# Block transposes over 128 partitions, with a trip through HBM that orders their rows

## The chip, the cores and the metric

The kernel runs on one core of one Trainium2 chip. TensorE (PE in the profile) does the matmuls, VectorE (DVE) and ScalarE (ACT) the elementwise work, GpSimd (POOL) here memsets and a few DMA issues, SyncE (SP) issues nearly all DMAs. The metric is the device time of one execution in microseconds (us). Three runs of the kernel before took 2368.86, 2369.55 and 2369.81 us; the median is 2369.55 us.

## The reference

Two models of two layers each run one after the other on one sequence of 256 tokens with 1024 channels, all in float32. Every layer is a half-weighted SwiGLU feed-forward network (FFN), a mixer with attention, and a second FFN; each begins with an RMS norm. There are eight FFNs in all, and they hold most of the work:

```
def swiglu(x, w_in, w_out):            # w_in: 1024 x 5632, w_out: 2816 x 1024
    g, u = jnp.split(x @ w_in, 2, axis=-1)
    return (jax.nn.silu(g) * u) @ w_out

for l in range(DEPTH):                 # the first model; the second has another mixer
    x = x + 0.5 * swiglu(rms_norm(x, ffn1_norm[l]), ffn1_w_in[l], ffn1_w_out[l])
    x = x + mixer(rms_norm(x, mix_norm[l]), ...)    # q, k, v = h @ w_in: attention, and a Fourier branch
    x = x + 0.5 * swiglu(rms_norm(x, ffn2_norm[l]), ffn2_w_in[l], ffn2_w_out[l])
```

## The kernel before

Tokens lie on the partitions: x is one tile of 128 partitions x 2 token halves (t) x 1024 channels. A matmul needs the channels on the partitions, so the activations are transposed and then split into two parts, hi (rounded to fp32r) and lo (the remainder): xhi and xlo for x, hhi and hlo for the hidden layer h of an FFN. ACT makes hi, DVE makes lo (`split`, L313). Weights are split in the same way while they stream in, and every product is three matmuls, hi x hi, lo x hi and hi x lo (`mm3`, L112 to L116).

`unit` (L80) loads 1 MB of weights (4 blocks of 128 rows x 512 columns) into a `raw` buffer, of which there are four, and splits it in two halves of 128x1024 elements: whi on ACT (L315), wlo on DVE (L316). Such a half feeds 12 matmuls of 512 columns (2 row blocks x 2 token halves x 3). Inside an FFN four halves can be held at a time: two buffers of the pools `whi` and `wlo`, and two more that `more(2)` grants.

An FFN (`ffn`, L218) goes through six column blocks c of the hidden layer (the last is half as wide). For each it does the gate and the up product (16 weight blocks), then ACT takes the silu (L246) and DVE the product h (L248). h is transposed in four groups that begin at the blocks 0, 2, 4 and 5, with 8, 8, 4 and 2 pieces of 128 channels (nk). `queue_t` (L65) puts the transposes of a group and then its splits into a list, `todo`. `unit` takes up to `rate` = 4 entries from it after each weight half and ties them behind that half's wlo on DVE (L104 to L106); `drain` takes all that are left.

`queue_blocks` (L179) does the transposes: DVE transposes 32x32 blocks within 32 partitions, so each instruction reads 32 partitions of the source and writes 32 partitions of the target at the place where the block belongs; that makes 16 instructions of 32 partitions x nk*32 elements for each token half, 32 for a group. For the first 512 channels of x after an FFN `queue_x` (L170) does the same with nk = 4; the other 512 are transposed on PE (`xt_half`, L187). In the first model's mixer (`mixer1`, L418) q and k are transposed in this way too, into qT and kT (L456), and are split after the four projections (L470 to L474).

The tile framework orders the instructions of each engine from a simulated timeline; each engine then works strictly in that order. hhi goes to ACT's list, hlo and wlo to DVE's.

Of the kernel before, what the change touches and what calls it, by code (L numbers as in the profile page):

```python
# [10 lines left out]
F32 = mybir.dt.float32  # L11
# [7 lines left out]
P = 128  # L19
T = 2  # L20
# [6 lines left out]
class Net:  # L27
    def __init__(self, tc, ctx, a):
        self.tc, self.nc, self.a = tc, tc.nc, a
        nc = self.nc  # L30
        pool = lambda n, b, **kw: ctx.enter_context(tc.tile_pool(name=n, bufs=b, **kw))
# [9 lines left out]
        self.at = pool("at", 4, space=PS)  # L41
        self.tp = pool("tp", 1, space=PS)
        self.uid = 0
        self.flip = False
# [13 lines left out]
        self.hold = False  # L58
        self.todo, self.rate = [], 4

# [4 lines left out]
    def queue_t(self, h, nk, hhi, hlo, k0):  # L65
        hv = self.b("hT", n=2048)[:, : nk * 256].rearrange("p (k t) -> p k t", k=nk)
        for t in range(T):
            self.queue_blocks(h[t], nk, hv, t)
        for i in range(0, nk, 2):
            self.todo.append(lambda i=i: self.split(hhi[:, k0 + i : k0 + i + 2], hlo[:, k0 + i : k0 + i + 2],  # L70
                                                    hv[:, i : i + 2]))

# [97 lines left out]
    def queue_x(self, li):  # L170
        nc = self.nc
        hv = self.xtile()[:, :1024].rearrange("p (k t) -> p k t", k=4)
        for t in range(T):
            self.queue_blocks(self.x[:, t, :512], 4, hv, t)
        for k in range(4):
            g = self.gcol[:, li, k : k + 1] if isinstance(li, int) else li[:, k : k + 1]
            self.todo.append(lambda k=k, g=g: self.split(self.xhi[:, k], self.xlo[:, k], hv[:, k], scale=g))

    def queue_blocks(self, src, nk, hv, t):  # L179
        src = src.rearrange("p (k c i) -> p k c i", c=4, i=32)  # L180
        for q in range(16):
            qa, qc = q // 4, q % 4
            self.todo.append(lambda qa=qa, qc=qc: self.nc.vector.transpose(  # L183
                (hv(qc) if callable(hv) else hv)[32 * qc : 32 * qc + 32, :, t * P + 32 * qa : t * P + 32 * qa + 32],
                src[32 * qa : 32 * qa + 32, :nk, qc, :]))

# [196 lines left out]
class Mix1:  # L383
# [34 lines left out]
    def mixer1(self, l, nxt):  # L418
        nc, a, tc = self.nc, self.a, self.tc
# [3 lines left out]
        big = self.big  # L423
        self.more(2)
        tl = lambda n, sh, dt=F32: big.tile(sh, dt, name=self.nm(n), tag="m1" + n)
        kzh = big.tile([P, 4, 2, 256], F32R, name=self.nm("kzh"), tag="mlo")
        kq = big.tile([P, 4096], F32R, name=self.nm("kq"), tag="m1th")
        kzl = kq[:, :2048].rearrange("p (k i t) -> p k i t", k=4, i=2)
        ql = kq[:, 2048:3072].rearrange("p (k t) -> p k t", k=4)
        qT = big.tile([P, 4, 256], F32, name=self.nm("qT"), tag="m1fhi")  # L430
        kT = big.tile([P, 4, 256], F32, name=self.nm("kT"), tag="m1flo")
        qh, vn = tl("qh", [P, 4, 256], F32R), tl("vn", [P, T, 512])
# [6 lines left out]
        for c in range(4):  # L439
# [5 lines left out]
            if c < 2:  # L445
                h = []
                for t in range(T):
# [6 lines left out]
                    h.append(ht)  # L454
                for t in range(T):
                    self.queue_blocks(h[t], 4, qT if c == 0 else kT, t)  # L456
            elif c == 2:
# [12 lines left out]
        self.drain()  # L470
        self.split(qh, ql, qT)
        for i in range(2):
            r = slice(64 * i, 64 * i + 64)
            self.split(kzh[r, :, i, :], kzl[r, :, i, :], kT[r])  # L474
        ohi, olo = tl("ohi", [P, 4, 256], F32R), tl("olo", [P, 4, 256], F32R)
# [19 lines left out]
        for g in range(4):  # L495
            pa = self.psum(self.at)
            for tt in range(T):
                s = slice(g * P, (g + 1) * P)
# [5 lines left out]
            for q in range(2):  # L504
                s = slice(q * P, (q + 1) * P)
# [9 lines left out]
        for c in range(4):  # L515
# [4 lines left out]
            for t in range(T):  # L520
                d = th[:, t, c * 512 : (c + 1) * 512]
# [618 lines left out]
```

## Time and profile before

| | |
|---|---|
| runs, median of 3 | 2369.55 us (2368.86 to 2369.81) |
| profiled execution, its span | 2366.5 us |
| between the two | 3.05 us outside the span or from run to run; the profile has no other time of its own |
| PE busy | 2291.0 us, 97% of the span |
| DVE busy | 1891.9 us, 80% |
| ACT busy | 1144.7 us, 48% |
| POOL busy | 22.3 us, 1% |
| DMA | 407.07 MB, mean 172 GB/s; 16 engines busy about half of the time |

The span runs from the first to the last instruction of the profiled execution. A busy PE is not a PE at its full rate: an instruction's bar lasts 0.39 us, while the starts of two matmuls of 512 columns are 0.23 us apart where nothing is late. So what PE loses is read from its waits and from the number of matmuls in a stretch, not from the busy share. DVE's share is an average too: it differs a good deal between stretches.

### The profile page before, as it was taken

Reading aid. Unit: us, or ns where it says so; the run is one execution under the profiler, and the core shown is the slowest. Engines: PE = TensorE matmul, PEld = TensorE weight load, DVE = VectorE, ACT = ScalarE, POOL = GpSimd, SP = SyncE. Lnnn points to the kernel's source line nnn. Section 1 sums busy time; section 2 is a strip of 40 time slices with the busy share of each in tenths; the row PEclk is TensorE's granted clock in tenths of the full one; section 3 lists DMA queues with packets and bytes.
Section 4 is the critical chain, followed back from the end, with each engine's and each line's share of the span. In section 5 each row is a group of like instructions: output and inputs, shape, how many; then the busy total and the mean of one; then the engine's idle time right before and its main releaser. Section 6 shows DMA issues by size and latency. Waiting matters only on the chain.

```text
span 2366.5 us, 28600 instructions
## 1 busy us (share of the span) xinstructions
PE 2291.0 (97%) x10446; PEld 1846.8 (78%) x10446; DVE 1891.9 (80%) x3797; ACT 1144.7 (48%) x1632; POOL 22.3 (1%) x47
## 2 busy tenths in 40 slices
PE   8999999999999999999999999999999999999999
PEld 7777788778778788777777887787787788778777
DVE  6898866896798876798788896768958978877785
ACT  5444445445444455445444655544444455455443
POOL 0000000000000000000000000000000000000000
PEclk9999999999999999999999999999999999999999
DMA  7555555556546645546555544455464555325553
GB/s 257 177 171 185 177 170 178 173 174 201 182 151 200 191 152 178 189 142 219 176 175 179 174 125 132 137 185 182 166 211 161 173 191 156 124 96 189 185 177 117
DMA packets 228269, 407.07 MB, mean 172 GB/s; under 512 B 20800, under 2 KB 46016, under 8 KB 228128
## 3 DMA queue, kind: packets, MB, share of 16 engines
q1 hardware_dynamic: 212272, 397.44, 51.0%
q10 hardware_dynamic: 14944, 4.79, 0.9%
q0 software_dynamic: 912, 3.02, 0.5%
q8 instruction: 82, 1.34, 0.2%
q14 instruction: 59, 0.48, 0.1%
HBM read 404.16 MB, written 1.05 MB: 171 GB/s over the span
## 4 chain that ended last, share of the span: by engine, by line
PE 66%; DVE 27%; issue 5%; ACT 2%; DMA 1%; ACTq 0%; DVEq 0%
PE ps L115 20%; PE ps L116 20%; PE ps L114 19%; DVE hT L183 14%; DVE wlo L316 8%; DVE h L248 2%; PE ps L377 2%; DVE hlo L316 1%; ACT whi L315 1%; PE ps L370 1%; PE ps L863 1%; DVE qT L183 1%; PE ps L655 1%; DMA raw<-in_mix_w_in_dram 1%; PE ps L194 1%
## 5 line engine op out<-in xcount | busy, mean ns | idle before, releaser
L315 ACT CAST whi<-raw 128x1024 fp32r<-128x1024 f32 (+2 forms) x754 | 780.2, 1043 | 834.4 <-PE ps L116 744.8
L316 DVE TENSOR_TENSOR wlo<-raw,whi 128x1024 fp32r<-128x1024 f32 (+2 forms) x754 | 907.6, 1213 | 337.1 <-ACT whi L315 323.6
L115 PE MATMUL ps<-wlo,xhi 128*128 128x512 f32 (+2 forms) x2048 | 804.6, 394 | 14.7 <-DVE wlo L316 14.7
L114 PE MATMUL ps<-whi,xhi 128*128 128x512 f32 (+2 forms) x2048 | 772.4, 394 | 22.1 <-DVE h L248 18.9
L116 PE MATMUL ps<-whi,xlo 128*128 128x512 f32 (+2 forms) x2048 | 791.2, 390 | 0.0
L114 PEld LDWEIGHTS ps<-whi,xhi 128*128 128x128 f32 x2048 | 383.4, 188 | 112.7 <-DVE h L248 25.7
L115 PEld LDWEIGHTS ps<-wlo,xhi 128*128 128x128 f32 x2048 | 384.8, 188 | 110.5 <-DVE wlo L316 31.2
L116 PEld LDWEIGHTS ps<-whi,xlo 128*128 128x128 f32 x2048 | 384.8, 188 | 79.3 <-issue 0.5
L183 DVE STREAM_TRANSPOSE hT<-h 32x256 f32<-32x256 f32 (+2 forms) x1024 | 360.8, 352 | 15.4
L115 PE MATMUL ps<-wlo,hhi 128*128 128x512 f32 x704 | 279.1, 396 | 23.7 <-DVE wlo L316 23.7
L116 PE MATMUL ps<-whi,hlo 128*128 128x512 f32 x704 | 275.8, 392 | 0.0
L114 PE MATMUL ps<-whi,hhi 128*128 128x512 f32 x704 | 266.2, 392 | 1.1 <-DVE h L248 0.2
L115 PEld LDWEIGHTS ps<-wlo,hhi 128*128 128x128 f32 x704 | 132.1, 188 | 65.2 <-DVE wlo L316 37.5
L114 PEld LDWEIGHTS ps<-whi,hhi 128*128 128x128 f32 x704 | 132.2, 188 | 33.7 <-DVE h L248 4.6
L116 PEld LDWEIGHTS ps<-whi,hlo 128*128 128x128 f32 x704 | 132.2, 188 | 27.8
L315 ACT CAST hhi<-hT 128x512 fp32r<-128x512 f32 x88 | 49.1, 618 | 119.1 <-DVE hT L183 119.1
L246 ACT ACTIVATE sl<-ps,rstd 128x512 f32<-128x512 f32 (+1 forms) x96 | 62.3, 651 | 56.4 <-PE ps L116 52.3
L183 DVE STREAM_TRANSPOSE hT<-x 32x128 f32<-32x128 f32 x224 | 67.7, 302 | 3.4
L365 ACT ACTIVATE pr<-ms,nmx 128x256 f32<-128x256 f32 (+1 forms) x112 | 51.3, 461 | 34.0 <-DVE nmx L360 29.9
L248 DVE SCALAR_TENSOR_TENSOR h<-ps,rstd,sl 128x512 f32<-128x512 f32 (+1 forms) x96 | 64.7, 700 | 1.9 <-PE ps L116 1.6
L316 DVE TENSOR_TENSOR hlo<-hT,hhi 128x512 fp32r<-128x512 f32 x88 | 55.7, 685 | 0.3
L137 ACT ACTIVATE jk<-x 128x512 f32<-128x512 f32 x52 | 32.7, 630 | 5.3 <-DVE x L299 2.6
(350 smaller groups left out, 1681.7 us busy)
## 6 DMA issues: line engine op xcount, KB each, us to landing
raw<-in_ffn_w_gu_dram SPq DMA_DIRECT2D x80, 1024.0 KB, 5.1
raw<-in_ffn_w_in_dram SPq DMA_DIRECT2D x79, 1024.0 KB, 5.2
raw<-in_ffn_w_out_dram SPq DMA_DIRECT2D x40, 1024.0 KB, 5.0
raw<-in_ffn_w_down_dram SPq DMA_DIRECT2D x40, 1024.0 KB, 5.1
raw<-in_mix_w_in_dram SPq DMA_DIRECT2D x32, 1024.0 KB, 6.7
raw<-in_w_gate_dram SPq DMA_DIRECT2D x24, 1024.0 KB, 5.1
raw<-in_w_in_dram SPq DMA_DIRECT2D x12, 1024.0 KB, 5.5
raw<-in_ffn_w_in_dram SPq DMA_DIRECT2D x16, 512.0 KB, 4.6
```

The source lines that it names most:

```text
L114: mm(ps[:, :n], lhsT=lh, rhs=hi, start=start, stop=False)
L115: mm(ps[:, :n], lhsT=lh, rhs=lo, start=False, stop=False)
L116: mm(ps[:, :n], lhsT=ll, rhs=hi, start=False, stop=stop)
L137: self.nc.scalar.activation(junk, self.x[:, t, n * 512 : (n + 1) * 512], AF.Square, accum_out=ss[:, t, n : n + 1])
L183: self.todo.append(lambda qa=qa, qc=qc: self.nc.vector.transpose((hv(qc) if callable(hv) else hv)[32 * qc : 32 * qc + 32, :, t * P + 32 * ...
L194: nc.tensor.transpose(ps[:, j * 256 + t * P : j * 256 + (t + 1) * P], self.x[:, t, k * P : (k + 1) * P], self.ident)
L246: nc.scalar.activation(sl[:, :w], gs[t][:, :w], AF.Silu, scale=rs[:, t : t + 1])
L248: nc.vector.scalar_tensor_tensor(h[t][:, o : o + w], us[t][:, :w], rs[:, t : t + 1], sl[:, :w], op0=ALU.mult, op1=ALU.mult)
L315: self.nc.scalar.copy(hi, src)
L316: return self.nc.vector.tensor_sub(lo, src, hi.bitcast(F32))
L365: nc.scalar.activation(pr[:, s], src[:, s], AF.Exp, bias=nm[:, j : j + 1], accum_out=den[:, j : j + 1])
L377: nc.tensor.matmul(po[:, j * 64 : (j + 1) * 64], lhsT=pt[:, q], rhs=v(j, st), start=(st == 0), stop=(st == ns - 1))
```

## The change

The 16 transposes of 32 partitions for each token half become one instruction over all 128 partitions (`turn` in the new function `turned`, which takes the place of `queue_blocks`). It transposes each 32x32 block where it stands: the four quarters of the token half stay in their own 32 partitions, and the channels are taken with a step of four elements. What it writes, a tile hB, has the right elements in the wrong partitions. Two DMAs issued on POOL's queue put that right: the first writes hB to a buffer in HBM (`hop`), the second reads it back with the rows in order into the tile that the transposes wrote before (hT, qT or kT). Both move 1 MB for nk = 8, 512 KB for nk = 4 and 256 KB for nk = 2.

hT then has its columns in another order (quarter, piece, token half), and the splits read it in runs of 32 elements, one token half at a time, four pieces at a time: as many splits as before for nk = 8 and nk = 4, two of half the width in place of one for nk = 2, eight of 128x128 in place of four of 128x256 for x, and twice as many of half the width for q and k. `rate` goes from 4 to 1, and empty entries in the list (two for h, three for x) leave weight halves between the transposes and the splits.

```
@@ -40,6 +40,7 @@
         self.acc = pool("acc", 3, space=PS)
         self.at = pool("at", 4, space=PS)
         self.tp = pool("tp", 1, space=PS)
+        self.hop = pool("hop", 2, space=bass.MemoryType.DRAM)
         self.uid = 0
         self.flip = False
         self.ident = self.cst.tile([P, P], F32, name="ident")
@@ -56,19 +57,38 @@
         self.extra = self.turn = 0
         self.lead = True
         self.hold = False
-        self.todo, self.rate = [], 4
+        self.todo, self.rate = [], 1
 
     def drain(self):
         while self.todo:
             self.todo.pop(0)()
 
     def queue_t(self, h, nk, hhi, hlo, k0):
-        hv = self.b("hT", n=2048)[:, : nk * 256].rearrange("p (k t) -> p k t", k=nk)
-        for t in range(T):
-            self.queue_blocks(h[t], nk, hv, t)
-        for i in range(0, nk, 2):
-            self.todo.append(lambda i=i: self.split(hhi[:, k0 + i : k0 + i + 2], hlo[:, k0 + i : k0 + i + 2],
-                                                    hv[:, i : i + 2]))
+        hv = self.turned(lambda t: h[t], nk, self.b("hT", n=2048))
+        self.todo += [lambda: None] * 2
+        step = min(nk, 4)
+        for i in range(0, nk, step):
+            for t in range(T):
+                o = lambda d: d[:, k0 + i : k0 + i + step, t * P : (t + 1) * P].rearrange(
+                    "p k (q j) -> p k q j", j=32)
+                self.todo.append(lambda hi=o(hhi), lo=o(hlo), s=hv[:, i : i + step, t]: self.split(hi, lo, s))
+
+    def turned(self, src, nk, tile):
+        nc = self.nc
+        n = nk * 256
+        hop = self.hop.tile([4, P, nk * 64], F32, name=self.nm("hop"), tag=f"hop{nk}")
+        hb = self.b("hB", n=2048, bufs=1)[:, :n]
+        ov = hb.rearrange("p (c k t j) -> p k c t j", c=4, t=T, j=32)
+
+        def turn(t):
+            nc.vector.transpose(ov[:, :, :, t, :], src(t)[:, : nk * P].rearrange("p (k i c) -> p k c i", c=4, i=32))
+            if t == T - 1:
+                nc.gpsimd.dma_start(out=hop.rearrange("q (i c) n -> (q i) (c n)", c=4), in_=hb)
+                nc.gpsimd.dma_start(out=tile[:, :n].rearrange("p (q n) -> p q n", q=4),
+                                    in_=hop.rearrange("q p n -> p q n"))
+
+        self.todo += [lambda t=t: turn(t) for t in range(T)]
+        return tile[:, :n].rearrange("p (q k t j) -> p k t q j", q=4, t=T, j=32)
 
     def nm(self, s):
         self.uid += 1
@@ -168,21 +188,16 @@
         return r
 
     def queue_x(self, li):
-        nc = self.nc
-        hv = self.xtile()[:, :1024].rearrange("p (k t) -> p k t", k=4)
-        for t in range(T):
-            self.queue_blocks(self.x[:, t, :512], 4, hv, t)
-        for k in range(4):
+        hv = self.turned(lambda t: self.x[:, t, :512], 4, self.xtile())
+        self.todo += [lambda: None] * 3
+
+        def part(k):
             g = self.gcol[:, li, k : k + 1] if isinstance(li, int) else li[:, k : k + 1]
-            self.todo.append(lambda k=k, g=g: self.split(self.xhi[:, k], self.xlo[:, k], hv[:, k], scale=g))
-
-    def queue_blocks(self, src, nk, hv, t):
-        src = src.rearrange("p (k c i) -> p k c i", c=4, i=32)
-        for q in range(16):
-            qa, qc = q // 4, q % 4
-            self.todo.append(lambda qa=qa, qc=qc: self.nc.vector.transpose(
-                (hv(qc) if callable(hv) else hv)[32 * qc : 32 * qc + 32, :, t * P + 32 * qa : t * P + 32 * qa + 32],
-                src[32 * qa : 32 * qa + 32, :nk, qc, :]))
+            for t in range(T):
+                o = lambda d: d[:, k, t * P : (t + 1) * P].rearrange("p (q j) -> p q j", j=32)
+                self.split(o(self.xhi), o(self.xlo), hv[:, k, t], scale=g)
+
+        self.todo += [lambda k=k: part(k) for k in range(4)]
 
     def xt_half(self, n, li):
         nc = self.nc
@@ -427,8 +442,8 @@
         kq = big.tile([P, 4096], F32R, name=self.nm("kq"), tag="m1th")
         kzl = kq[:, :2048].rearrange("p (k i t) -> p k i t", k=4, i=2)
         ql = kq[:, 2048:3072].rearrange("p (k t) -> p k t", k=4)
-        qT = big.tile([P, 4, 256], F32, name=self.nm("qT"), tag="m1fhi")
-        kT = big.tile([P, 4, 256], F32, name=self.nm("kT"), tag="m1flo")
+        qT = big.tile([P, 1024], F32, name=self.nm("qT"), tag="m1fhi")
+        kT = big.tile([P, 1024], F32, name=self.nm("kT"), tag="m1flo")
         qh, vn = tl("qh", [P, 4, 256], F32R), tl("vn", [P, T, 512])
         u = big.tile([P, KD, 256], F32R, name=self.nm("u"), tag="mhi").rearrange("p (h t a) b -> p h t (a b)", h=2, t=2)
         uhi, ulo = u[:, 0], u[:, 1]
@@ -452,8 +467,8 @@
                     else:
                         nc.vector.tensor_scalar(out=ht, in0=ps[t], scalar1=sc, scalar2=None, op0=ALU.mult)
                     h.append(ht)
-                for t in range(T):
-                    self.queue_blocks(h[t], 4, qT if c == 0 else kT, t)
+                turned = self.turned(lambda t, h=h: h[t], 4, qT if c == 0 else kT)
+                qv, kv = (turned, None) if c == 0 else (qv, turned)
             elif c == 2:
                 for t in range(T):
                     sc = rs[:, t : t + 1]
@@ -468,10 +483,12 @@
                     nc.vector.scalar_tensor_tensor(ulo[:, t], ps[t], sc, uhi[:, t].bitcast(F32),
                                                    op0=ALU.mult, op1=ALU.subtract)
         self.drain()
-        self.split(qh, ql, qT)
-        for i in range(2):
-            r = slice(64 * i, 64 * i + 64)
-            self.split(kzh[r, :, i, :], kzl[r, :, i, :], kT[r])
+        for t in range(T):
+            o = lambda d: d[:, :, t * P : (t + 1) * P].rearrange("p k (q j) -> p k q j", j=32)
+            self.split(o(qh), o(ql), qv[:, :, t])
+            for i in range(2):
+                r = slice(64 * i, 64 * i + 64)
+                self.split(o(kzh[:, :, i])[r], o(kzl[:, :, i])[r], kv[r, :, t])
         ohi, olo = tl("ohi", [P, 4, 256], F32R), tl("olo", [P, 4, 256], F32R)
         for p in range(4):
             if p % 2 == 0:
```

The names below are the tiles with their numbers: wlo and whi are halves of weights, h_333 to h_336 the two token halves of a group of h, hT its transposed form.

DVE, in the first FFN, from the first transpose of the first group (before the change):

```order
L183 STREAM_TRANSPOSE hT_487<-h_333 32x8x32 x12
L316 TENSOR_TENSOR wlo_543<-raw_532,whi_542 128x1024
L183 STREAM_TRANSPOSE hT_487<-h_333 32x8x32 x4
L316 TENSOR_TENSOR wlo_579<-raw_576,whi_578 128x1024
L183 STREAM_TRANSPOSE hT_487<-h_334 32x8x32 x4
L316 TENSOR_TENSOR wlo_587<-raw_576,whi_586 128x1024
L183 STREAM_TRANSPOSE hT_487<-h_334 32x8x32 x4
L316 TENSOR_TENSOR wlo_621<-raw_618,whi_620 128x1024
L183 STREAM_TRANSPOSE hT_487<-h_334 32x8x32 x4
L316 TENSOR_TENSOR wlo_629<-raw_618,whi_628 128x1024
L183 STREAM_TRANSPOSE hT_487<-h_334 32x8x32 x4
L316 TENSOR_TENSOR wlo_673<-raw_670,whi_672 128x1024
```

The same place on DVE after the change:

```order
L84 STREAM_TRANSPOSE hB_491<-h_335 128x8x4x32
L331 TENSOR_TENSOR wlo_539<-raw_532,whi_538 128x1024
L84 STREAM_TRANSPOSE hB_491<-h_336 128x8x4x32
L331 TENSOR_TENSOR wlo_571<-raw_568,whi_570 128x1024
L331 TENSOR_TENSOR wlo_577<-raw_568,whi_576 128x1024
L331 TENSOR_TENSOR wlo_609<-raw_606,whi_608 128x1024
L331 TENSOR_TENSOR wlo_615<-raw_606,whi_614 128x1024
L331 TENSOR_TENSOR wlo_657<-raw_654,whi_656 128x1024
L331 TENSOR_TENSOR hlo_151<-hT_489,hhi_150 128x4x128 x4
L331 TENSOR_TENSOR wlo_661<-raw_654,whi_660 128x1024
L263 SCALAR_TENSOR_TENSOR h_644<-ps_566,rstd_306,sl_646 128x512
L331 TENSOR_TENSOR wlo_691<-raw_688,whi_690 128x1024
```

Of the 32 transposes two are left, and between the second of them and the four hlo stand five weight halves; before, wlo_685 also stood ahead of the four hlo, which followed wlo_673.

ACT at the same place, before (whi_672 and whi_684 are the halves of wlo_673 and wlo_685):

```order
L315 CAST whi_628<-raw_618 128x1024
L246 ACTIVATE sl_665<-ps_489,rstd_304 128x512
L315 CAST whi_672<-raw_670 128x1024
L315 CAST whi_684<-raw_670 128x1024
L315 CAST hhi_148<-hT_487 128x512 x4
L315 CAST whi_714<-raw_712 128x1024
```

And after:

```order
L330 CAST whi_614<-raw_606 128x1024
L261 ACTIVATE sl_649<-ps_493,rstd_306 128x512
L330 CAST whi_656<-raw_654 128x1024
L330 CAST hhi_150<-hT_489 128x4x128 x4
L330 CAST whi_660<-raw_654 128x1024
L330 CAST whi_690<-raw_688 128x1024
```

The four hhi, which wait for hT, now stand one weight half earlier, ahead of whi_660.

POOL from the start of the program before, up to the first mixer's gate biases (L518):

```order
masks.py:199 AFFINE_SELECT ident<-ident 128x128
L323 MEMSET kzh_1617 64x4x256
L324 MEMSET kzh_1617 64x4x256
L323 MEMSET kq_1618 64x4x256
L324 MEMSET kq_1618 64x4x256
L518 DMA h_2440<-in_mix_gate_bias_dram 128x512
```

After, from the end of the first FFN (hop_1049 is the group with nk = 2, hop_1257 is x) to the same place:

```order
L86 DMA hop_1049<-hB_1050 128x512
L87 DMA hT_1048<-hop_1049 128x4x128
L86 DMA hop_1257<-hB_1258 128x1024
L87 DMA hT_1256<-hop_1257 128x4x256
L338 MEMSET kzh_1499 64x4x256
L339 MEMSET kzh_1499 64x4x256
L338 MEMSET kq_1500 64x4x256
L339 MEMSET kq_1500 64x4x256
L86 DMA hop_1619<-hB_1620 128x1024
L87 DMA qT_1501<-hop_1619 128x4x256
L535 DMA h_2276<-in_mix_gate_bias_dram 128x512
```

86 DMAs are new in POOL's list, two for each of 43 transposed tiles: 32 of h, 7 of x, 4 of q and k.

## Rows read from the trace of the kernel before

**Rows 1.** The page: busy time of each engine.
```profile
PE 2291.0 (97%) x10446; PEld 1846.8 (78%) x10446; DVE 1891.9 (80%) x3797; ACT 1144.7 (48%) x1632; POOL 22.3 (1%) x47
```

**Rows 2.** The page: the chain that ended last, by line.
```profile
PE ps L115 20%; PE ps L116 20%; PE ps L114 19%; DVE hT L183 14%; DVE wlo L316 8%; DVE h L248 2%; PE ps L377 2%; DVE hlo L316 1%; ACT whi L315 1%; PE ps L370 1%; PE ps L863 1%; DVE qT L183 1%; PE ps L655 1%; DMA raw<-in_mix_w_in_dram 1%; PE ps L194 1%
```

**Rows 3.** Busy time by stretches: from:to, length, engines' us and instructions, clock, DMA.
```profile
20.00:52.00 32.00, 32.00 (x143) 26.49 (x142) 18.31 (x28) 17.07 (x19) 0.00 (x0) 1.00 0.73 246
54.00:84.00 30.00, 28.34 (x123) 22.38 (x122) 29.33 (x50) 13.77 (x17) 0.00 (x0) 1.00 0.53 172
...
130.00:160.00 30.00, 26.69 (x113) 20.50 (x112) 28.78 (x76) 11.42 (x14) 0.00 (x0) 1.00 0.36 123
165.00:190.00 25.00, 25.00 (x112) 20.71 (x111) 22.34 (x48) 12.22 (x18) 0.00 (x0) 1.00 0.53 160
213.00:256.00 43.00, 38.16 (x161) 29.32 (x160) 41.18 (x85) 19.50 (x22) 2.29 (x4) 1.00 0.52 149
```

**Rows 4.** PE's waits: total us, times, longest.
```profile
PE ps L115 <- DVE wlo L316: 38.4, 57, 1.7
PE ps L114 <- DVE h L248: 19.0, 17, 1.2
```

**Rows 5.** PE's timeline: start, us, instruction, in brackets the wait before it.
```profile
61.77 0.84 PE L114 MATMUL ps<-whi,xhi 128*128 128x512 f32 x3
...
79.24 0.39 PE L114 MATMUL ps<-whi,xhi 128*128 128x512 f32 x1
80.78 0.50 PE L114 MATMUL ps<-whi,xhi 128*128 128x512 f32 x1 [1.15 <-DVE h L248]
```

**Rows 6.** Groups of instructions by shape: busy us, mean ns, idle before.
```profile
L316 DVE TENSOR_TENSOR wlo<-raw,whi 128x1024 fp32r<-128x1024 f32 x734 | 890.8, 1223 | 334.7 <-ACT whi L315 321.4
L183 DVE STREAM_TRANSPOSE hT<-h 32x256 f32<-32x256 f32 x512 | 223.0, 435 | 7.7
L183 DVE STREAM_TRANSPOSE hT<-h 32x128 f32<-32x128 f32 x256 | 77.4, 302 | 3.8
L183 DVE STREAM_TRANSPOSE hT<-x 32x128 f32<-32x128 f32 x224 | 67.7, 302 | 3.4
L183 DVE STREAM_TRANSPOSE hT<-h 32x64 f32<-32x64 f32 x256 | 60.4, 236 | 3.8
...
L316 DVE TENSOR_TENSOR hlo<-hT,hhi 128x512 fp32r<-128x512 f32 x88 | 55.7, 685 | 0.3
...
L183 DVE STREAM_TRANSPOSE kT<-h 32x128 f32<-32x128 f32 x64 | 19.4, 303 | 1.0
```

**Rows 7.** DVE's timeline in the first FFN, at the first group of h.
```profile
53.32 1.40 DVE L248 SCALAR_TENSOR_TENSOR h<-ps,rstd,sl 128x512 f32<-128x512 f32 x2
54.64 5.37 DVE L183 STREAM_TRANSPOSE hT<-h 32x256 f32<-32x256 f32 x12
...
77.57 2.49 DVE L316 TENSOR_TENSOR hlo<-hT,hhi 128x512 fp32r<-128x512 f32 x4
```

**Rows 8.** ACT: the weight half by shape, and the four hhi in its timeline.
```profile
L315 ACT CAST whi<-raw 128x1024 fp32r<-128x1024 f32 x734 | 765.3, 1051 | 819.9 <-PE ps L116 730.3 <-DMA raw<-in_mix_w_in_dram 37.2 <-DVE hT L183 18.8
...
75.29 2.19 ACT L315 CAST hhi<-hT 128x512 fp32r<-128x512 f32 x4 [4.11 <-DVE hT L183]
```

**Rows 9.** DMA issues: count, KB each, median us from issue to landing.
```profile
raw<-in_ffn_w_gu_dram SPq DMA_DIRECT2D x80, 1024.0 KB, 5.1
...
h<-in_mix_gate_bias_dram POOLq DMA_DIRECT2D x8, 256.0 KB, 4.1
...
gf<-in_final_norm_dram POOLq DMA_DIRECT2D x1, 512.0 KB, 4.1
out_dram<-x ACTq DMA_DIRECT2D x2, 256.0 KB, 3.4
```

**Rows 10.** POOL's timeline: a memset and a DMA issue of 128 rows.
```profile
199.86 0.95 POOL L323 MEMSET kzh<- 64x1024 f32 x1 [198.56 <-PE ps L116]
...
232.67 0.54 POOL L518 DMA_DIRECT2D h<-in_mix_gate_bias_dram  x1 [9.70 <-DVE qT L183]
```

**Rows 11.** ACT's waits from 213 to 256 us, in the first mixer.
```profile
ACT whi L315 <- DMA raw<-in_mix_w_in_dram: 11.2, 2, 10.1
```

## The prediction

> **What bounds the kernel now.** I read the page's busy shares first, then the chain, then the same shares by stretch, and last who waits for whom. The page alone misleads: PE is busy for 97% of the span and DVE for 80% [rows 1], as if PE set the time alone. The chain has PE at about 60% in its three matmul lines, but also 14% on DVE's transposes of h and 8% on wlo [rows 2]: somewhere DVE ends last. The stretches tell where. From 20 to 52 us, where nothing is transposed, PE starts 143 matmuls in 32 us, 4.47 per us; from 54 to 84 us, with the transposes of the first group of h, only 123 in 30 us, and DVE is busy for 29.33 of the 30 [rows 3]. There DVE is the bound. The clock is 1.00 in all stretches, the level of 2.4 GHz, so it plays no part.
>
> How much PE loses, counted in two ways:
> - By stretches [rows 3]: at 4.47 per us, 54 to 84 lacks 11 matmuls (2.5 us). The second group of this FFN is the same again. 130 to 160, with the last two groups of h, lacks 21 (4.7 us). 165 to 190, with x, lacks none. An FFN loses 9.7 us, eight of them 78 us. In the first model's mixer, 213 to 256, 31 are missing, 6.9 us, twice. Sum: 92 us.
> - By waits [rows 4]: 38.4 us for wlo and 19.0 us for h, 74 waits. A wait is counted only after the modelled end of the matmul before it. In [rows 5] the starts at 79.24 and 80.78 are 1.54 us apart where 0.23 is normal, a loss of 1.31, and the wait shows 1.15; the slow matmul behind it costs another 0.11. So add 0.27 to each: 57.4 + 74 x 0.27 = 77 us.
>
> So 77 to 92 us, 85 in the middle, is the most that a lighter DVE can give back.
>
> **The change, part by part.** *Transposes removed:* 223.0 + 77.4 + 67.7 + 60.4 us, and 19.4 each for qT and kT: 467 us of DVE [rows 6].
>
> *Transposes added.* The rows give 236, 302 and 435 ns for 64, 128 and 256 elements [rows 6], so 1.04 ns per element and 0.17 us fixed, for 32 partitions. If all 128 partitions run side by side, 1024 elements take 1.23 us, 512 take 0.70, 256 take 0.44. 32 + 38 + 16 of these (h with nk = 8; nk = 4 of h, x, q and k; nk = 2) are 39 + 27 + 7 = 73 us. If the four quarters ran one after the other, 1024 elements would take 16 x 0.435 = 7 us, and nothing would change. No row shows a transpose over 128 partitions; I take side by side, since the other operations over 128 partitions cost the same per element (1223 - 685 ns for 512 elements more, 1.05 ns [rows 6]).
>
> *Splits.* As many elements as before, in more instructions for x, q, k and the last group; some 7 us of fixed cost on DVE, spread over stretches that then have slack. DVE as a whole: 1892 - 467 + 73 + 7 = 1505 us. In 54 to 84: 29.3 - 13.9 + 2.5 = 17.9 of 30 us. That stretch goes back to PE's pace, if the new trip isn't late.
>
> *The trip.* It is what may be late next. One leg of 512 KB on POOL's queue lands after 4.1 us, as one of 256 KB does [rows 9]. By size, 1024 KB on SP against 256 KB out to HBM differ by 1.7 us for 768 KB [rows 9], so 1 MB on POOL is 4.1 + 1.1 = 5.2 us. Two legs and the waits between them: 10.6 us. Against it: the weights take some 53% of the DMA engines in these stretches [rows 3], so a leg that meets a weight load shares with it, up to 2.6 us each (about half of 5.1), and the second leg reads 512 rows of 2 KB where the rows show issues of 128 (0.54 us [rows 10]); if the issue goes by rows, 4 x 0.54, it is 1.6 us more. Bounds 10.6 and 17.4 us; I take 13, near the lower, as the weights load in bursts with pauses.
>
> The Trainium skill ("DMA: Bandwidth & Descriptors", section Anatomy of one DMA) says that completion can be surprisingly late when the target is HBM. Here a store of 256 KB to HBM lands after 3.4 us and a load of 256 KB on POOL after 4.1 [rows 9], so the trace doesn't bear it out; by the page's fit, 2.0 us and bytes over 436 GB/s, two legs would be an estimated 8.8 us.
>
> *When it must be there.* At the first group DVE finishes h at 54.6 [rows 7]; then come transpose, wlo, transpose: 54.64 + 1.23 + 1.22 + 1.23 = 58.4 us. In the new order hhi stands on ACT ahead of whi_660, so a late trip holds up whi_660 and wlo_661. PE takes up the weight half of the first wlo behind h at 61.77 [rows 5]; five halves and the first token half of a sixth later, at 61.8 + 5.5 x 2.7 = 76.7, it needs wlo_661. Back from there: wlo 1.22, whi 1.05, four hhi 2.19 [rows 6, 8]: hT must land by 72.2. That allows the trip 13.8 us from the second transpose. At 13 it is just in time; each microsecond beyond 13.8 is one that PE stands still, in each of the 16 groups with nk = 8. The groups with nk = 4 and 2 have legs of 4.1 us, 8.4 together, and four weight halves (10.9 us) or three (8.2 us) between transposes and splits; ACT's lead over PE covers a microsecond or two there. What I lose to late trips and to the four hlo in a row (2.49 us [rows 7]): 0.7 us in 16 groups (11 us), 0.7 us at each of eight FFN ends (6 us).
>
> *Mixer.* DVE is busy for 41.2 of 43 us and 64 of its transposes (19.4 us) go. Part of the loss is ACT waiting 11.2 us for a weight load [rows 11], which in turn waited for a raw buffer that DVE freed late. That gets better, but the trips of q and k load the DMA engines there; I keep 2.5 us of the 6.9, twice: 5 us.
>
> *POOL's queue* is in order, and some of its instructions wait long: a memset of kzh for 198.56 us [rows 10]. In the new order the trips of an FFN stand ahead of the next mixer's memsets, so they are not held up. q's trip stands behind these memsets, which end well before.
>
> **The sum.** 85 - 11 - 6 - 5 = 63 us. The span goes from 2366.5 to 2303.5 us; the median of the runs lies 3.05 us above the span before, and I keep that: 2306.5 us.
>
> **The rivals.**
> - *The trip is 2 to 3 us later than I take it*, because it meets a weight load in both legs. Then each of the 16 groups loses 2 us to ACT in place of 2.5 to DVE. Left are the FFN ends, 8 x 4, and the mixers, 2 x 3, about 35 us: 2335. For it: the DMA share of 0.53; against it: the weight loads have four raw buffers and can themselves be put off.
> - *The step of four elements slows the transposes.* The sources are read with 16 bytes between elements; no row shows such a read. If each element took two cycles, 1024 elements would last 2.3 us, and the trip would start 2.2 us later. With my 13 us, hT lands 1.3 us late: 16 x 1.3 = 21 us less gain, 2328. The Trainium skill ("SBUF — State Buffer", section Door 1: The DMA port swizzle) says that every access which crosses to a new line of 16 bytes pays, which is this case; the same note calls a step of four float32 free. By its first sentence this rival would hold, by the second my forecast; no row here decides.
> - *The trip becomes the bound, and the kernel is slower.* Place: hhi on ACT ahead of whi_660, 16 times. Each group loses the trip's time over 13.8 us, and the groups with smaller legs lose along with it (their two trips at an FFN's end take some 80% as long, against 8 to 11 us of distance). All groups together reach the 85 us at trips of about 18 us; at 21 us it is 16 x 7.2 + 8 x 6 = 163 against 85, so 2448. For it: the issue by rows and two weight loads at once, which give 17.4. Against it: both bounds must hold at the same time.
> - *Nothing gets faster*, as the four quarters run in turn: 2370.
>
> **How the numbers follow.** Forecast 0.62, own range 2282 to 2322. Late by 2 to 3 us 0.16, step of four 0.10, trip as the bound 0.08, nothing 0.04. Less than 0.2%, 4.7 us, can't be told from no change. Faster: 0.62 + 0.16 + 0.10 = 0.88, a little less, 0.87, for trips near 18 us that give all of it back; same 0.05; slower 0.08. The range runs from the whole 85 us (2284) to the late trip with some of its own spread (2348); outside are the slow cases and a little at the lower end.
>
> **What would show it.** Right: in the stretches with transposes DVE is busy for about 60%, and PE starts 4.4 per us; the transposes over 128 partitions last about 1.2 us; PE's waits for wlo and h fall from 57 us to under 15; DVE's total is near 1500 us. The trip: from the issue of the first leg to the landing of the second, 12 to 14 us. Wrong: ACT's waits for a DMA into hT ahead of hhi, followed by PE waiting for whi and wlo, in every group with nk = 8. A transpose of 2.3 us speaks for the step, one of 5 us and more for the quarters in turn.

## The result and the profile after

The changed kernel takes 2293.09 us (median of 4 runs, 2290.19 to 2300.69) against 2369.2 us (2368.51 to 2369.81) in the same comparison: a ratio of 0.9682, 95% interval 0.9671 to 0.9694. That is 76 us less where 63 were forecast, and inside the range. The profiled execution has a span of 2292.5 us; before it was 2366.5, so the two profiles differ by 74.0 us.

Busy time of each engine and the chain by line, from the page (to be read against [rows 1] and [rows 2]):

```profile
PE 2271.5 (99%) x10446; PEld 1859.0 (81%) x10446; DVE 1548.3 (68%) x2549; ACT 1148.6 (50%) x1674; POOL 78.1 (3%) x133
...
PE ps L135 20%; PE ps L136 20%; PE ps L134 20%; DMA hT<-hop 2%; DMA hop<-hB 1%; PE ps L392 1%; DVE wlo L331 1%; DVE hlo L331 0%; PE ps L209 0%; DMA rawb<-in_rpbp_dram 0%; ACT whi L330 0%; PE ps L385 0%; DMA raw<-in_mix_w_in_dram 0%; PE ps L229 0%; DMA x<-in_x_dram 0%
```

DVE loses 344 us of work, and the 14% of the chain that stood on its transposes are gone; 3% on the two legs of the trip are new. The same stretches as in [rows 3]:

```profile
20.00:52.00 32.00, 32.00 (x143) 26.51 (x142) 17.24 (x29) 16.80 (x19) 0.00 (x0) 1.00 0.74 250
54.00:84.00 30.00, 30.00 (x134) 24.86 (x133) 22.00 (x21) 14.74 (x17) 1.44 (x2) 1.00 0.74 254
130.00:160.00 30.00, 30.00 (x134) 24.86 (x133) 17.33 (x20) 13.78 (x18) 2.06 (x3) 1.00 0.71 243
165.00:190.00 25.00, 25.00 (x112) 20.70 (x111) 13.62 (x18) 11.62 (x17) 0.98 (x2) 1.00 0.64 180
213.00:256.00 43.00, 43.00 (x207) 35.71 (x206) 33.16 (x58) 24.31 (x40) 3.90 (x7) 1.00 0.91 277
```

Read the numbers in brackets behind PE: 134 matmuls in 30 us where 123 and 113 were, 4.47 per us, the pace of the stretch without transposes. x, which lost nothing, still loses nothing. DVE is busy for 73% of the stretch from 54 to 84 us and 58% of the one from 130 to 160; the prediction's sign was about 60%. The DMA engines are busier (0.74 for 0.53). PE's waits, against [rows 4]:

```profile
PE ps L135 <- DVE wlo L331: 5.4, 9, 0.8
PE ps L134 <- ACT whi L330: 2.8, 5, 1.1
```

The line for whi in the kernel before, which [rows 4] leaves out:

```profile
PE ps L114 <- ACT whi L315: 3.5, 6, 1.5
```

57.4 us of waits for wlo and h have become 5.4; those for whi were 3.5 us and are 2.8. Counted another way, by the starts of PE's matmuls (each gap less the usual one, 0.23 us for 512 columns), PE lost 143.4 us before and 69.4 after; the difference is the 74.0 us of the spans. By the place in the program: the eight FFNs lost 78 us and now 14, the first model's two mixers 15.3 and now 3.8; the rest, the start and the second model's mixers, is 50 us and now 52.

The new instructions, by shape (busy us, mean ns, idle before), and the DMA issues (count, size, median us to landing):

```profile
L84 DVE STREAM_TRANSPOSE hB<-h 128x1024 f32<-128x1024 f32 x32 | 64.0, 1999 | 0.0
L84 DVE STREAM_TRANSPOSE hB<-h 128x512 f32<-128x512 f32 x24 | 25.0, 1082 | 0.0
L331 DVE TENSOR_TENSOR hlo<-hT,hhi 128x512 fp32r<-128x512 f32 x80 | 50.3, 687 | 33.3 <-ACT hhi L330 33.1
```

```profile
hop<-hB POOLq DMA_DIRECT2D x16, 1024.0 KB, 5.6
hT<-hop POOLq DMA_DIRECT2D x16, 1024.0 KB, 6.2
...
hop<-hB POOLq DMA_DIRECT2D x19, 512.0 KB, 4.0
...
hT<-hop POOLq DMA_DIRECT2D x15, 512.0 KB, 4.5
```

A transpose of 1024 elements takes 2.00 us, not 1.23: 1.79 ns for each element more (1999 - 1082 over 512) in place of 1.04. The trip in the first group, on POOL and ACT:

```profile
61.67 0.68 POOL L86 DMA_DIRECT2D hop<-hB  x1 [60.37 <-DVE hB L84]
67.47 0.76 POOL L87 DMA_DIRECT2D hT<-hop  x1 [5.13 <-DMA hop<-hB]
...
73.62 2.19 ACT L330 CAST hhi<-hT 128x512 fp32r<-128x512 f32 x4 [0.73 <-DMA hT<-hop]
```

From the first issue to hhi it is 12.0 us. ACT waits 0.73 us for the landing, and PE waits for nothing. The group at 579 us is the worst of the 16:

```profile
581.66 0.55 POOL L86 DMA_DIRECT2D hop<-hB  x1 [73.18 <-issue]
588.30 0.76 POOL L87 DMA_DIRECT2D hT<-hop  x1 [6.10 <-DMA hop<-hB]
...
596.20 2.18 ACT L330 CAST hhi<-hT 128x512 fp32r<-128x512 f32 x4 [3.62 <-DMA hT<-hop]
```

```profile
599.38 0.49 PE L134 MATMUL ps<-whi,xhi 128*128 128x512 f32 x1 [1.09 <-ACT whi L330]
600.64 0.50 PE L135 MATMUL ps<-wlo,xhi 128*128 128x512 f32 x1 [0.77 <-DVE wlo L331]
600.97 0.56 PE L136 MATMUL ps<-whi,xlo 128*128 128x512 f32 x1
601.33 0.63 PE L134 MATMUL ps<-whi,xhi 128*128 128x512 f32 x1
601.76 0.63 PE L135 MATMUL ps<-wlo,xhi 128*128 128x512 f32 x1
```

Here the trip takes 14.5 us, ACT waits 3.62, and PE stands still twice. Behind the stall the matmuls start 0.43 us apart for 3 us: the granted clock is at its lower level there (0.51 from 601.0 to 604.2 us). In 4 of the 16 groups PE waits like this, in the other three for 0.5 to 0.8 us at trips of 13.4 to 13.7 us; in the other 12 the wlo behind the splits is ready 0.1 to 1.1 us ahead of PE. (The expectations below speak of five late groups; the fifth is 0.12 us ahead.) So the trips have no reserve to speak of.

### The profile page after: what moved, and what is told of

The parts are those of the page before. It is cut to its first block, busy times and chain, and to the rows that moved or that the text cites. A ratio compares the mean times of both kernels' runs of the same rounds, so it can differ in the third digit from the quotient of the medians.

```text
span 2292.5 us, 27621 instructions
## 1 busy us (share of the span) xinstructions
PE 2271.5 (99%) x10446; PEld 1859.0 (81%) x10446; DVE 1548.3 (68%) x2549; ACT 1148.6 (50%) x1674; POOL 78.1 (3%) x133
## 4 chain that ended last, share of the span: by engine, by line
PE 62%; issue 32%; DMA 4%; DVE 1%; ACT 1%; POOLq 0%; ACTq 0%; POOL 0%; DVEq 0%
PE ps L135 20%; PE ps L136 20%; PE ps L134 20%; DMA hT<-hop 2%; DMA hop<-hB 1%; PE ps L392 1%; DVE wlo L331 1%; DVE hlo L331 0%; PE ps L209 0%; DMA rawb<-in_rpbp_dram 0%; ACT whi L330 0%; PE ps L385 0%; DMA raw<-in_mix_w_in_dram 0%; PE ps L229 0%; DMA x<-in_x_dram 0%
## 5 line engine op out<-in xcount | busy, mean ns | idle before, releaser
L134 PE MATMUL ps<-whi,xhi 128*128 128x512 f32 (+2 forms) x2048 | 787.2, 393 | 2.6 <-ACT whi L330 2.3
L134 PE MATMUL ps<-whi,hhi 128*128 128x512 f32 x704 | 272.6, 391 | 0.0
L84 DVE STREAM_TRANSPOSE hB<-h 128x1024 f32<-128x1024 f32 (+2 forms) x72 | 99.2, 1390 | 1.2 <-DMA hop<-hB 1.0
L331 DVE TENSOR_TENSOR hlo<-hT,hhi 128x512 fp32r<-128x512 f32 (+1 forms) x96 | 57.0, 643 | 53.5 <-ACT hhi L330 53.2
L330 ACT CAST hhi<-hT 128x512 fp32r<-128x512 f32 (+1 forms) x96 | 49.8, 582 | 80.3 <-DMA hT<-hop 80.3
L86 POOL DMA_DIRECT2D hop<-hB x43 | 23.5, 547 | 1756.2 <-DVE hB L84 747.0
L87 POOL DMA_DIRECT2D hT<-hop x39 | 29.5, 757 | 185.6 <-DMA hop<-hB 101.0
```

What stands on the lines that cost most here:

```text
L84: nc.vector.transpose(ov[:, :, :, t, :], src(t)[:, : nk * P].rearrange("p (k i c) -> p k c i", c=4, i=32))
L86: nc.gpsimd.dma_start(out=hop.rearrange("q (i c) n -> (q i) (c n)", c=4), in_=hb)
L87: nc.gpsimd.dma_start(out=tile[:, :n].rearrange("p (q n) -> p q n", q=4), in_=hop.rearrange("q p n -> p q n"))
L134: mm(ps[:, :n], lhsT=lh, rhs=hi, start=start, stop=False)
L330: self.nc.scalar.copy(hi, src)
L331: return self.nc.vector.tensor_sub(lo, src, hi.bitcast(F32))
```

## The experiments

The theory after the result: the gain is DVE's time in stretches where DVE was the bound, and the trip is hidden where hT lands ahead of the slot of its splits. The rivals: the new order of the list makes the gain; the trip still costs much; the step of four costs time.

### The step of four

```
-src(t)[:, : nk * P].rearrange("p (k i c) -> p k c i", c=4, i=32)
+src(t)[:, : nk * P].rearrange("p (k c i) -> p k c i", c=4, i=32)
```

> The transposes read channels in contiguous runs of 32 in place of a step of four; the two DMAs stay as they are, so the channels of h, x, q and k end up in another order (this part of the computation is changed). Theory (the gain is DVE no longer being the bound; the trip is hidden while hT lands before the slot of its splits): a transpose of 1024 elements falls from 2.00 us to about 1.23, of 512 from 1.08 to 0.70, of 256 from 0.64 to 0.44; DVE's total falls by some 43 us, to about 1505. The trips start 1.5 us earlier, the few PE stalls behind late trips go (about 5 us), the rest of the time does not move: 2284 to 2293. Rival (the step of four costs 16 x 1.3 us of the gain, as my prediction had it): about 2272. If the slow transposes are not due to the step, they stay at 2.0 us and the time stays at 2293.

Measured: 2288.5 us (2284.56 to 2295.69), ratio 0.9671 (0.9658 to 0.9685). The transposes, by shape:

```profile
L84 DVE STREAM_TRANSPOSE hB<-h 128x1024 f32<-128x1024 f32 x32 | 39.5, 1236 | 0.0
L84 DVE STREAM_TRANSPOSE hB<-h 128x512 f32<-128x512 f32 x24 | 15.6, 687 | 0.0
```

The step is what makes them slow: without it they last 1.236 and 0.687 us, as forecast for side by side, and DVE's total is 1506 us, the forecast 1505. The time is 4.6 us less, with intervals that overlap, not the 21 us of the rival.

### No trip at all

Both `dma_start` are left out, and the transposes write to the tile that the splits read. The order is made anew, with one weight half between the second transpose of a group and its splits.

> Both DMAs of the trip are left out and the splits read what the transposes wrote, rows out of order (this part of the computation is left out). The splits move forward, since nothing waits for a landing. Theory (the trip is hidden but for the 5 late groups): 2284 to 2291. Rival (the trip and its 58 MB more of DMA still cost much, for instance by delaying weights): below 2280. DVE busy unchanged at about 1548 us.

Measured: 2285.72 us (2284.89 to 2286.01), ratio 0.9647 (0.9634 to 0.9661). So the whole trip costs some 7 us of time. It may be some 4 more, since in the order made for this kernel the last mixer takes 3.6 us longer than in the changed kernel, with a wait that the latter has not:

```profile
PE ps L129 <- ACT oTc L225: 2.1, 1, 2.1
```

The trips' 58 MB of traffic, then, cost little.

### A longer trip that the order knows of

```
                 nc.gpsimd.dma_start(out=hop.rearrange("q (i c) n -> (q i) (c n)", c=4), in_=hb)
+                nc.gpsimd.dma_start(out=hop2, in_=hop)
                 nc.gpsimd.dma_start(out=tile[:, :n].rearrange("p (q n) -> p q n", q=4),
-                                    in_=hop.rearrange("q p n -> p q n"))
+                                    in_=hop2.rearrange("q p n -> p q n"))
```

> A third DMA on POOL's queue, between the two legs, copies the block from HBM to HBM, so that every trip is one leg of about 5 to 6 us longer and moves half as much again. The order is made anew: for nk = 8 the splits now stand 8 weight halves behind the second transpose, in place of 5. Theory (only a trip that is late for the slot of its splits costs): distance 12.9 + 3 x 2.72 = 21 us against a trip of about 18, so it is hidden: 2285 to 2296. Rival (the deadline stands still, as my prediction wrote it, and 5 us more of trip cost 5 us in each of 16 groups): about 2370. Rival (29 MB more read and written slow the weights): slower by more than 5 us without waits for hlo.

Measured: 2285.58 us (2283.62 to 2285.84), ratio 0.9647 (0.9632 to 0.9661). The first group, on POOL and ACT:

```profile
59.83 0.69 POOL L87 DMA_DIRECT2D hop<-hB  x1 [58.53 <-DVE hB L85]
65.70 0.52 POOL L88 DMA_DIRECT2D hop<-hop  x1 [5.18 <-DMA hop<-hB]
71.69 0.80 POOL L89 DMA_DIRECT2D hT<-hop  x1 [5.47 <-DMA hop<-hop]
...
77.70 2.19 ACT L332 CAST hhi<-hT 128x512 fp32r<-128x512 f32 x4 [1.20 <-DMA hT<-hop]
```

The trip is 5.9 us longer (17.9 us), moves half as much again, and the kernel is 7.5 us faster than the changed one. The order is made from a simulated timeline, and with the length of the trip the place of the splits moves: 1 weight half behind the second transpose without a trip, 5 with two legs, 8 with three. That they stand where the simulation has hT land fits this; the simulated times themselves are not on record. In 15 of the 16 groups wlo is now ready 2.8 to 3.3 us ahead of PE. So the deadline is not a property of the kernel: it moves with a trip that the order knows of, and what costs time here is how far the real trip comes behind the place that the order gave it.

### The splits of h held to a place

Here the splits of a group with nk = 8 are one entry behind `e` empty ones, and ACT's copies from there on (four hhi and the next eight) are held in program order. e = 8, 4, 5, 6 and 9 put 7, 3, 4, 5 and 8 weight halves between the second transpose and the splits.

```
+        if nk == 8:
+            self.todo += [lambda: None] * e
+            self.todo.append(four)          # sets self.pin = 12, then the four splits
+            return
...
+            if self.pin:
+                self.pin -= 1
+                self.tc.add_manual_dep(c.ins, self.prev, ...)   # order alone, no wait
```

Seven halves:

> In the 16 groups with nk = 8 the splits of h are held to a fixed place in ACT's and DVE's order, 7 weight halves behind the second transpose in place of 5; nothing else changes. Theory (a group costs time only where its trip is late for the slot; in the profile after, 5 of the 16 groups leave wlo behind the splits only 0.05 us ahead of PE, the others 0.4 to 1.1 us): two halves are 5.4 us more of distance, all 16 are early, the stalls of about 1 to 2 us in those 5 groups go: 2286 to 2290. Rival (the trip costs nothing at all now, the stalls have another cause): 2293. Rival (splits that come later block a buffer): slower than 2293.

Three halves:

> As the run with 7 halves, but with 3 weight halves between the second transpose and the splits of h in the 16 groups, in place of 5. Theory (deadline as predicted, each microsecond beyond it is lost in each of the 16 groups): the deadline comes 2 x 2.72 = 5.4 us earlier, the slack in the profile after adds up to 9 us over the groups, so 16 x 5.4 - 9 = 78 us slower: about 2371, near the kernel before. PE waits for wlo behind hlo in all 16 groups, some 5 us each. Rival (ACT waits but PE has enough halves in hand, or catches up later): 2293 to 2310.

Four halves:

> As the runs with 3 and 7 weight halves between the second transpose and the splits of h, with 4 halves. Theory: 16 x 2.72 less the 9 us of slack in the profile after = 35 us slower than after, 2328; where the stalls are followed by matmuls at the clock's lower level, as behind those of 3.6 us in the run with 3 halves (8 matmuls 0.20 us late each, 1.6 us), up to 16 x 1.6 = 26 us more, 2354. Rival (no price below a stall of some us): about 2295.

Five halves, the place in the changed kernel:

> As before with 5 halves, which is where the changed kernel has its splits of h: a control for the fixing itself. Theory: 2290 to 2297, as the changed kernel. Rival (the fixed place, not the distance, made the runs with 7 halves faster): about 2285.

Eight halves:

> As before with 8 halves. Theory: with 7 halves no group was late any more, so nothing is left to gain: 2282 to 2287. Rival (each half of distance gives some more): below 2281. Rival (the splits block the next group's tiles): above 2290.

| halves | median us | ratio, 95% interval | lost in the 16 groups, us |
|---|---|---|---|
| 3 | 2390.92 | 1.0084 to 1.0111 | 67 |
| 4 | 2379.34 | 1.0026 to 1.0060 | 27 |
| 5, held | 2329.53 | 0.9809 to 0.9847 | 15 |
| 5, as changed | 2293.09 | 0.9671 to 0.9694 | 8 |
| 7 | 2284.58 | 0.9629 to 0.9655 | 2.6 |
| 8 | 2290.9 | 0.9653 to 0.9681 | 2.9 |

The last column adds PE's gaps beyond the usual one from 4 us behind a group's second transpose to 6 us behind PE's first use of the wlo that follows the splits. It goes the way of the theory: with 7 halves nothing is left to lose (0.3 us in each of the last eight groups is there in every run), with 3 every group loses 2.5 to 6.2 us. The size is smaller: 19 us more than in the changed kernel with 4 halves, where 35 were expected, and 59 with 3, where 78 were. The theory took a half for 2.72 us; by the semaphores that PE waits for in the first FFN, its first uses of successive halves are 2.7, 1.4, 1.4 and 5.4 us apart in turn. In the first group one half less moves the deadline by 1.4 us, and two by 4.1. PE in the first group with 3 halves, and the stretch behind the stall (the last columns are clock, DMA share and GB/s):

```profile
73.12 0.39 PE L150 MATMUL ps<-whi,xlo 128*128 128x512 f32 x1
77.12 1.74 PE L148 MATMUL ps<-whi,xhi 128*128 128x512 f32 x3 [3.62 <-ACT whi L344]
78.66 0.63 PE L149 MATMUL ps<-wlo,xhi 128*128 128x512 f32 x1
```

```profile
77.20:80.30 3.10, 3.10 (x7) 2.32 (x8) 3.10 (x3) 2.71 (x3) 0.00 (x0) 0.50 0.30 46
```

The starts are 4.00 us apart, and then 7 matmuls start in 3.1 us at a granted clock of 0.50 (1.2 GHz), where 14 would.

The medians don't follow from that column alone. The control with 5 halves was expected at 2293 and came out 36 us above it, so the fixing itself costs time. The stretches of the first group and of the FFN's end, with 5 halves held:

```profile
54.00:84.00 30.00, 30.00 (x134) 24.86 (x133) 22.02 (x21) 14.74 (x17) 1.44 (x2) 1.00 0.74 253
130.00:160.00 30.00, 27.43 (x120) 22.10 (x119) 16.03 (x19) 12.73 (x16) 2.35 (x4) 1.00 0.56 200
```

The group that was moved is at full pace; 130 to 160 us, with the groups of nk = 4 and 2, lacks 14 matmuls, 3.1 us, and the other FFNs' ends lose about as much. PE stands still there for a whi that follows the hhi of the nk = 4 group on ACT (1.7 us) and for its wlo (0.8 us). With 4 halves the same stretch starts 99 matmuls and loses 7.8 us. The empty entries push these groups back in the list, and the eight copies that are held include theirs. That this is the reason, and why it doesn't show with 7 and 8, no run tells. The clock adds to it: its mean is 0.983 with 3 halves and 0.985 with 4, for 0.998 in the changed kernel, as stretches at the lower level follow the longer stalls. So the gap column speaks for the deadline; the medians with 3, 4 and 5 halves held are not its price (with 3 halves 59 of the 98 us above the changed kernel lie in the groups, 39 elsewhere). With 8 halves the median is 4 us above the expected range. In its profile the groups lose nothing, so it is not the splits blocking a tile; 3.9 us are lost in the second layer's mixer of the second model, half of them in a wait that the run with 7 halves has not, the others at the clock's lower level behind it:

```profile
PE ps L148 <- ACT oTc L244: 2.1, 1, 2.1
```

Seven halves, 2284.58 us, has the lowest median of all. That it is the distance and not the fixing, the longer trip speaks for: with nothing held it has the same time.

### The order of the list alone

The kernel before gets the changed kernel's `rate` of 1 and its empty entries, and `queue_blocks` puts the 16 old transposes of a token half into one entry; there is no trip.

```
-        self.todo, self.rate = [], 4
+        self.todo, self.rate = [], 1
...
+        self.todo.append(lambda: [four(qa) for qa in range(4)])
```

> The transposes of before (32 partitions each, no trip) in the list of after: the 16 of one token half are one entry, entries come one for each weight half, with the empty entries. Theory (the gain is the DVE time of the transposes): DVE's total is about 1890 again and the time 2365 to 2385, since 16 transposes in a row hold up wlo by 7 us. Rival (the gain comes from the new order of the list, one entry for each half and the splits apart from the transposes): about 2300.

Measured: 2555.24 us (2550.58 to 2556.82), ratio 1.0783 (1.0765 to 1.0801). DVE's timeline at the first group, PE's waits, and the stretch of [rows 3]:

```profile
55.40 14.36 DVE L203 STREAM_TRANSPOSE hT<-h 32x256 f32<-32x256 f32 x32
69.79 4.63 DVE L338 TENSOR_TENSOR wlo<-raw,whi 128x1024 fp32r<-128x1024 f32 x4
```

```profile
PE ps L134 <- DVE wlo L338: 195.9, 46, 7.7
```

```profile
54.00:84.00 30.00, 22.30 (x86) 17.84 (x85) 24.75 (x45) 10.64 (x13) 0.00 (x0) 0.83 0.42 139
```

With the old transposes this list is 186 us slower than before, more than the theory's 2365 to 2385, since all 32 transposes of a group come in a row and wlo stands behind them for 14.4 us, not 7. Behind such stalls the clock falls: it is 0.83 in this stretch and 0.958 in the whole run, and by the starts of the matmuls some 60 of the 186 us (an estimate) are lost at its lower level. So this run shows that the list alone gives nothing when the transposes stand in a row. One entry for each weight half, with four old transposes of h in an entry (and no empty entries for h), is in the kernel with x alone, below: 4.4 us slower than before. So the order doesn't make the gain.

### The parts

Each kernel keeps the new form for one of the three and the old transposes, four for each weight half, for the others:

```
-        hv = self.turned(lambda t: h[t], nk, self.b("hT", n=2048))
+        hv = self.b("hT", n=2048)[:, : nk * 256].rearrange("p (k t) -> p k t", k=nk)
+        for t in range(T):
+            self.queue_blocks(h[t], nk, hv, t)      # entries of four transposes
...
+        self.todo.append(s4)                        # all splits of the group
```

> Only h is transposed in the new way; x, q and k as before (four transposes for each weight half). Theory by the prediction's terms: the gain of h is what the FFN stretches lose, 76 of the 77 to 92 us less late trips, so 2369 less 62 to 70: 2299 to 2307, with x worth nothing. Rival (x or q and k carry much of the gain): above 2320.

> Only q and k of the first model's two mixers are transposed in the new way; h and x as before. Theory: each mixer loses 6.9 us in the profile before and gets back 4 to 7 of it, twice: 2355 to 2361. Rival (the loss there is the wait for the weights' DMA, which the trips make worse): 2365 to 2372.

> Only x is transposed in the new way; h, q and k as before. Theory: the stretch with x lost nothing before, so nothing changes: 2366 to 2371. Rival (h alone and q, k alone gave 60 and 4 us of 76, so the rest is x's): about 2358.

| new for | median us | ratio, 95% interval | against before |
|---|---|---|---|
| h | 2308.84 (2306.04 to 2314.99) | 0.9735 to 0.9765 | -60.4 |
| q, k | 2364.77 (2361.24 to 2366.42) | 0.9972 to 0.9990 | -4.4 |
| x | 2373.91 (2371.84 to 2375.14) | 1.0009 to 1.0028 | +4.4 |

The gain is h's, as the terms had it, though each part came out 2 to 4 us above its expected range, and together they give 60, not 76. The first mixer with q and k alone, and the FFN's end with x alone:

```profile
213.00:256.00 43.00, 43.00 (x193) 35.58 (x191) 33.77 (x58) 24.98 (x35) 4.86 (x8) 1.00 0.85 267
```

```profile
130.00:160.00 30.00, 26.21 (x111) 20.07 (x110) 28.87 (x75) 12.00 (x14) 0.00 (x0) 1.00 0.35 123
```

In the mixer PE is busy for all 43 us, so q and k do give back what was lost there (6.8 us in the first mixer, about 2 in the second). But where h is left old, each FFN's second half loses 0.4 us more than before (111 matmuls for 113), some 3 us in all: the old groups' splits are one entry in these kernels, which the kernel before didn't have. That corrects q and k to about -8 and x to about +1. With h alone the profile shows two late trips in the first FFN (ACT waits 3.80 us for hT at 120.86, PE loses 5.3 us in two groups). By the spans of the profiled executions (that of h alone is the slowest of its four) the parts fall 22 us short, and these have their places: 8 us the old groups in the two kernels without the new h, 9 in the FFNs with h alone, which have more late trips than the changed kernel, 3 in the first model's second mixer, the rest at the start and in the second model's mixers. Why h's trips are later when x, q and k are old, no run tells.

## Why the prediction was right

- *DVE is the bound in the stretches with transposes, 77 to 92 us, 85.* Right. 7 halves and the longer trip are 84 us faster than before; this is what a lighter DVE gives back. By place (the longer trip, first silu of an FFN to its last matmul) it is 9.9 or 10.0 us in each FFN of the first model, 8.1 or 8.2 in the second's, which I had taken like the first's, 12 in the two mixers together, and nothing at x.
- *The reserve of 22 us.* Mis-sized: 11 of the 13 us by which the forecast was off. Late trips were put at 11 us in the 16 groups, as 0.7 in each; they cost 5 to 6 us above the runs with more distance (8 against 2.6), in 4 groups. The 6 us at the FFN ends were 1, the 5 us in the mixers 3.8. The other 2 us are the 3.05 us that I kept between the profiled span and the median of the runs: here they lie 0.6 us apart.
- *Side by side: 1.23, 0.70 and 0.44 us.* The mechanism is right, the size was wrong for the operation as it stands: 2.00, 1.08 and 0.64, because of the step of four. Without the step they are as forecast. DVE's total is 1548 for 1505. That this error cost next to nothing is in part luck: the second transpose ends 1.5 us later than taken, and the trip behind it is 1 us shorter than taken.
- *The step as a rival, 21 us less gain.* Its premise holds: the Trainium skill ("SBUF — State Buffer", section Door 1: The DMA port swizzle) says that each access which crosses to a new line of 16 bytes pays; the trace agrees with that sentence (1.79 ns per element for 1.07 without the step), and not with the one that calls four float32 a free step; that it is the line and not the step as such, no run shows. The price fails: it was built on a trip of 13 us and 1.3 us of lateness in 16 groups; the trip took 12.0 in the first group, and without the step the time is 4.6 us less.
- *The trip, 13 us, 12 to 14 from issue to landing.* Right for most (11.5 to 14.5 in the 16 groups, ten of them within 12 to 14). The legs are 5.6 and 6.2 us for the 5.2 taken; the issue doesn't go by rows: 0.76 us for 512, 0.68 and 0.55 for 128.
- *The deadline of 13.8 us.* For the order on record it holds, and is 1 us too long: from the second transpose to the landing the first group takes 12.3 us and has 0.64 us left, 12.9 in all; trips of 13.4 to 13.7 us cost 0.8 to 1.1 us, the one of 14.5 us 4.0 with the clock. As a property of the change it is wrong. I read it as fixed by where hhi stands in the list; that place moves with the trip that the order knows of, and so a longer trip need not cost a microsecond for each of its own in 16 groups: one of 17.9 us costs nothing. With that the rivals "2 to 3 us later" and "the trip becomes the bound" had prices that only a delay unknown to the simulated timeline could have caused.
- *Clock.* I took it as 1.00 throughout. Behind starts 4.0 us apart (3 halves), and behind two gaps of 1.5 and 1.3 us in a row (the group at 579 us), come some 3 us at the lower level, in which PE loses 1.6 us more. With 5 halves held there is none behind gaps of 2.1 and 1.2 us at the end of the first FFN, and some 3 us at 0.50 behind gaps of 2.5 and 0.9 us at the end of the second: for stalls of this size the runs give no rule. That was in no term.

## What to carry to other kernels

Before costing a change, find the stretches where the engine is the bound and count the other engine's instructions in them: 85 us came from that count, and the runs gave 84. Where consumers are placed by a simulated timeline, a transfer that it knows of cost here by how far the real landing lay behind the place it gave; give it some slack (here two weight halves, 8 us gained) instead of shortening it. Never build an instruction sequence that holds one engine for longer than its consumer's buffers last: 32 small transposes in a row, at every group, cost 186 us that the same 32, spread over eight weight halves, did not.

## What was not expected of the hardware

- A 32x32 block transpose on DVE over 128 partitions takes 1.07 ns per element with contiguous runs and 1.79 ns with 16 bytes between elements; the quarters run side by side in both.
- The time to issue a DMA on POOL's queue grows little with its number of rows: 0.54 to 0.68 us for 128 rows of 8 KB, 0.76 for 512 rows of 2 KB. In the 16 groups a leg of 1 MB took 5.0 to 6.4 us (the first) and 5.6 to 8.1 (the second); whether the weight loads beside it make the difference was not tried.
- A small DMA on the queue of the trips is slower: the gate bias, 256 KB, lands after 6.7 us where it took 4.1 [rows 9]. That the trips of q and k beside it are the cause is not shown. No term had this, and PE doesn't wait for it.
